# A tiled matmul with bias and residual: one tile per ring slot for the whole kernel, in place of a new tile per use

## The chip, the cores and the metric

One core of a Trainium2 chip. The metric is the device time of one execution in microseconds. The kernel before took 210.93 us (median of 3 runs, 210.77 to 211.21). The span that a profile covers is shorter than the reported time (209.0 against 210.74 us).

## The reference

```python
x: (16, 512, 1024) float32; weight: (1024, 768); bias: (768,); residual: (16, 512, 768)
return (np.matmul(x, weight) + bias + residual).astype(np.float32)
```

Every byte has to move once. x is 33.55 MB, the residual 25.17, the weight 3.15 and the output 25.17, together 87.0 MB. The page of the profile counts 87.2 MB, so the kernel moves nothing twice.

## The kernel before

The 8192 rows of x are 64 row tiles of 128 rows, in 8 blocks of 8 tiles. For each row tile t, ScalarE casts x to bf16 (`xb`), TensorE transposes it as pairs packed in float32 (`pt`, in PSUM), VectorE copies that to SBUF (`xt`), TensorE does 8 contraction steps of two matmuls each (512 and 256 columns) into `po`, and VectorE adds the result to the residual, to which GpSimd has added or will add the bias. All large transfers are issued by SyncE.

Buffers that are used in turn are "rings". Each use of a slot asks the pool for a new tile with the slot's tag; the framework then makes the new tile wait until the old one is retired. A wait is a condition on a semaphore, a counter that other instructions raise. It rides on the instruction that needs it, or it is an instruction of its own, worked off in order by the engine's sequencer, the unit that hands the engine its instructions. A wait whose condition holds when it is reached is called met.

```python
J = 8; HEAD = 3; X_BUFS = 2; RO_BUFS = 4; TMP_BUFS = 4; EARLY = 24; T_STEP = 3
    sb = ctx.enter_context(tc.tile_pool(name="sb", bufs=1))
    ps = ctx.enter_context(tc.tile_pool(name="ps", bufs=1, space=bass.MemoryType.PSUM))

    def ring(pool, name, i, n, shape, dt):
        return pool.tile(shape, dt, name=name, tag=f"{name}{i % n}", bufs=1)

    def psum_o(i):
        return ring(ps, "po", i, HEAD, [P, N], FP32)

    def load_x(S, j0=0, j1=J):
        if S < n_s:
            if j0 == 0:
                x_sb[S] = ring(sb, "x_tile", S, X_BUFS, [P, J, K], FP32)
            K_(nc.sync.dma_start(out=x_sb[S][:, j0:j1, :], in_=x_d[S, :, j0:j1, :]))

    def load_res(S, j0=0, j1=J):
        if S < n_s:
            if j0 == 0:
                ro[S] = ring(sb, "ro", S, RO_BUFS, [P, J, N], FP32)
            K_(nc.sync.dma_start(out=ro[S][:, j0:j1, :], in_=res_d[S, :, j0:j1, :]))
    # [cut: load_w, store, cast]

    def transp(t):
        if t < n_t:
            pt = ring(ps, "pt", t, 2, [P, n_c, P], FP32)
            pairs = xb[t][:, :].bitcast(FP32)
            for c in range(n_c):
                K_(nc.tensor.transpose(
                    out=pt[:, c, :], in_=pairs[:, c * P:(c + 1) * P], identity=ident
                ))
            xt[t] = ring(sb, "xt", t, 4, [P, n_c, P], FP32)
            K_(nc.vector.tensor_copy(out=xt[t], in_=pt))

    def mms(t, i):
        if i == 0:
            po[t] = psum_o(t)
        for n0, nl in chunks:
            mm(t, i, n0, nl)
    # [cut: mm, pool_add, finish, the loads of the start and the first three row tiles]

    for t in range(HEAD, n_t):
        cast(t + 2)
        S, j = divmod(t, J)
        if (t + 2) % J == J - 1:
            if S == 0:
                load_x(X_BUFS, 0, J // 2)
                load_x(X_BUFS, J // 2, J)
            else:
                load_x(S + X_BUFS)
            load_res(S + X_BUFS)
            if 1 <= S < n_s - 1:
                store(S - 1)
        if t < n_t - 1:
            for i in range(len(steps)):
                mms(t, i)
                if i == 0 and t >= n_t - J // 2:
                    finish(t - 1)
                if i == T_STEP:
                    transp(t + 1)
        # [cut: finish, pool_add, the last stores and the last row tile]
```

Of the kernel before, what the change touches and what calls it, by code (L numbers as in the profile page):

```python
# [8 lines left out]
FP32 = mybir.dt.float32  # L9
BF16 = mybir.dt.bfloat16  # L10
P = 128
J = 8
HEAD = 3
X_BUFS = 2
RO_BUFS = 4
TMP_BUFS = 4
# [5 lines left out]
def kernel(  # L22
# [13 lines left out]
    N = weight.shape[1]  # L36
    n_c = K // (2 * P)
# [11 lines left out]
    sb = ctx.enter_context(tc.tile_pool(name="sb", bufs=1))  # L49
    ps = ctx.enter_context(tc.tile_pool(name="ps", bufs=1, space=bass.MemoryType.PSUM))  # L50

    def ring(pool, name, i, n, shape, dt):
        return pool.tile(shape, dt, name=name, tag=f"{name}{i % n}", bufs=1)

    def psum_o(i):
        return ring(ps, "po", i, HEAD, [P, N], FP32)

    x_sb, ro, xb, xt, po, tmp = {}, {}, {}, {}, {}, {}
# [3 lines left out]
# [11 lines that stand above are left out]
# [61 lines left out]
    bias_row = ring(sb, "tmp", TMP_BUFS - 1, TMP_BUFS, [P, N], FP32)  # L134
    K_(nc.gpsimd.memset(bias_row, 0.0))  # L135
    K_(nc.scalar.dma_start(out=bias_row[0:1, :], in_=bias[None, :]))
    w_st = ring(sb, "ro", RO_BUFS - 1, RO_BUFS, [P, n_c, 2, N], FP32)
    w_sb = const.tile([P, n_c, 2, N], BF16, name="w_sb")

    load_x(0, 0, 2)  # L140
# [13 lines left out]

    warm = const.tile([P, 512], BF16, name="warm")
    K_(nc.vector.memset(warm, 0.0))  # L156
    ones = ring(sb, "tmp", 0, TMP_BUFS, [P, P], FP32)
    K_(nc.vector.memset(ones, 1.0))
    warm_a = const.tile([1, 2], FP32, name="warm_a")
    K_(nc.vector.memset(warm_a, 0.0))  # L160
# [123 lines left out]
```

## Time and profile before

| | before |
|---|---|
| median time | 210.93 us |
| TensorE (PE) busy | 200.4 of 209.0 us |
| row tile period on PE, 20 to 199 us | 3.037 us |
| transfers, 20 to 180 us | 428 to 433 GB/s, busy share 1.00 to 1.01 |
| wait instructions on PE | 64 |

The page of the kernel before first: the busy time of PE, the busy share in tenths over 40 slices of the span for PE and for the DMA engines, the chain of waits that ended last, and two groups of instructions (after the bar: busy us, mean ns, idle us before).

```profile
PE 200.4 (96%) x1274; PEld 130.6 (63%) x1299; DVE 105.0 (50%) x139; ACT 67.6 (32%) x68; POOL 115.5 (55%) x71
...
PE   7999999999999999999999999999999999999980
...
DMA  6999999999999999999999999999999999999994
...
PE 96%; issue 1%; DVE 1%
...
L104 PE MATMUL po<-w_sb,xt 128*128 128x512 bf16 (+1 forms) x999 | 175.4, 324 | 1.4
...
L95 PE MATMUL pt<-ident,xb 128*128 128x128 f32 x256 | 38.2, 273 | 0.0
```

Two rows are full, PE and DMA.

The timeline of PE in the kernel before (start, duration, line, what, count):

```profile
98.77 2.76 PE L104 MATMUL po<-w_sb,xt 128*128 128x512 bf16 x16
101.37 0.60 PE L95 MATMUL pt<-ident,xb 128*128 128x128 f32 x4
101.81 2.76 PE L104 MATMUL po<-w_sb,xt 128*128 128x512 bf16 x15
```

From start to start a row tile takes 101.81 - 98.77 = 3.04 us: 2.60 for 16 matmuls, 0.44 for 4 transposes, no gap. (Recorded durations overlap. The x15 is a record lost from the trace: this trace has 1274 of 1299 matmuls.)

The windows of the kernel before, two stretches of 40 us (the last three columns are the granted clock, as a share of TensorE's full one, the DMA busy share and GB/s):

```profile
core 0: us, PE busy (x) PEld busy (x) DVE busy (x) ACT busy (x) POOL busy (x), PEclk, DMA share, GB/s
60.00:100.00 40.00, 39.74 (x261) 26.31 (x264) 20.75 (x28) 13.14 (x14) 30.28 (x17) 1.00 1.01 433
100.00:140.00 40.00, 39.74 (x260) 26.39 (x264) 20.75 (x27) 14.07 (x14) 25.10 (x16) 1.00 1.00 429
```

The instructions of the transpose's line in the kernel before: beside transposes and weight loads it has wait instructions, 51 ns each (a q after an engine's name marks what its sequencer does itself).

```profile
L95 PEldq EVENT_SEMAPHORE  x61: 51/51/51, 6.1 to 196.9; - x61
```

The timeline of SyncE before, from 14 to 24 us: the second residual block, then both halves of the third x block together, then the next residual.

```profile
14.19 0.33 SPq L72 DMA_DIRECT2D ro<-in_residual_dram  x1
22.54 0.81 SPq L66 DMA_DIRECT2D x_tile<-in_x_dram  x2
23.39 0.43 SPq L72 DMA_DIRECT2D ro<-in_residual_dram  x1
```

### The profile page before, as it was taken

How to read it: one execution, taken by the hardware profiler on the slowest of the kernel's cores; microseconds unless marked ns; L12 is line 12 of the kernel's file. 1: busy time of each engine (PE TensorE's matmuls, PEld its weight loads, DVE VectorE, ACT ScalarE, POOL GpSimd, SP SyncE). 2: the span in 40 equal slices, each digit the busy share in tenths (PEclk: the TensorE clock that was granted, in tenths of full speed). 3: DMA queues.
4: the chain of work that ended last, by engine and by line, in shares of the span. 5: the costliest groups of instructions: out<-in, count | busy, mean ns of one | idle time of the engine just before them, and what ended most of it. 6: DMA issues, size and time to landing. Idle time of an engine off the chain costs nothing.

```text
span 209.0 us, 3151 instructions
## 1 busy us (share of the span) xinstructions
PE 200.4 (96%) x1274; PEld 130.6 (63%) x1299; DVE 105.0 (50%) x139; ACT 67.6 (32%) x68; POOL 115.5 (55%) x71
## 2 busy tenths in 40 slices
PE   7999999999999999999999999999999999999980
PEld 2566666666666666666666666666666666666650
DVE  0737465445445544554554455455445544545550
ACT  2544315511723062422443054230724233430000
POOL 2000197819965565999189802994069910799000
PEclk9999999999999999999999999999999999999998
DMA  6999999999999999999999999999999999999994
GB/s 239 427 421 431 436 413 440 442 405 436 423 470 422 419 428 398 459 420 436 433 400 472 416 427 447 412 439 412 437 445 414 445 419 427 442 419 428 426 404 168
DMA packets 5632, 87.23 MB, mean 417 GB/s; under 512 B 625, under 2 KB 753, under 8 KB 1906
## 3 DMA queue, kind: packets, MB, share of 16 engines
q1 hardware_dynamic: 5616, 87.03, 97.9%
q8 instruction: 10, 0.16, 0.3%
q14 instruction: 4, 0.03, 0.0%
q10 hardware_dynamic: 2, 0.00, 0.0%
HBM read 61.87 MB, written 25.17 MB: 416 GB/s over the span
## 4 chain that ended last, share of the span: by engine, by line
PE 96%; issue 1%; DVE 1%
PE po L104 79%; PE pt L95 13%; PE po L170 3%; PE po L190 1%; DVE xt L99 0%; DVE ro L131 0%; DVE warm L156 0%
## 5 line engine op out<-in xcount | busy, mean ns | idle before, releaser
L104 PE MATMUL po<-w_sb,xt 128*128 128x512 bf16 (+1 forms) x999 | 175.4, 324 | 1.4
L104 PEld LDWEIGHTS <-xt 128*128 128x128 bf16 x1024 | 100.1, 98 | 59.5 <-DVE xt L99 0.5
L87 ACT CAST xb<-x_tile 128x1024 bf16<-128x1024 f32 x62 | 62.8, 1044 | 114.5 <-DMA x_tile<-in_x_dram 56.9
L121 POOL TENSOR_TENSOR ro<-ro,bias_sb 128x768 f32<-128x768 f32 x40 | 71.2, 1816 | 36.2 <-DMA ro<-in_residual_dram 26.2
L99 DVE COPY xt<-pt 128x512 f32<-128x512 f32 x64 | 44.2, 691 | 86.7 <-PE pt L95 86.5
L121 POOL TENSOR_TENSOR ro<-ro,tmp 128x768 f32<-128x768 f32 x24 | 43.1, 1814 | 41.0 <-DMA ro<-in_residual_dram 30.2
L131 DVE TENSOR_TENSOR ro<-po,ro 128x768 f32<-128x768 f32 (+2 forms) x41 | 38.0, 930 | 2.9 <-PE po L104 2.8
L95 PE MATMUL pt<-ident,xb 128*128 128x128 f32 x256 | 38.2, 273 | 0.0
L95 PEld LDWEIGHTS pt<-ident,xb 128*128 128x128 f32 x256 | 29.8, 141 | 8.1 <-issue 0.6
L129 DVE TENSOR_TENSOR tmp<-po,bias_sb 128x768 f32<-128x768 f32 x24 | 22.8, 949 | 0.6 <-POOL ro L121 0.5
L170 PE MATMUL po<-warm 128*128 128x512 bf16 x15 | 6.1, 579 | 1.2 <-DVE warm L156 1.2
L176 ACT CAST w_sb<-ro 128x768 bf16<-128x768 f32 x4 | 3.3, 832 | 4.0 <-DMA ro<-in_weight_dram 4.0
L170 PEld LDWEIGHTS <-warm 128*128 128x128 bf16 x15 | 1.9, 135 | 4.1 <-issue 2.8
L87 DVE CAST xb<-x_tile 128x1024 bf16<-128x1024 f32 x2 | 1.4, 696 | 4.8 <-DMA x_tile<-in_x_dram 4.8
L178 DVE CAST w_sb<-ro 128x768 bf16<-128x768 f32 x4 | 2.2, 555 | 2.5 <-DMA ro<-in_weight_dram 2.5
L161 ACT ACT_TABLE_LOAD x1 | 1.3, 1283 | 2.0 <-POOL ident masks.py:199 2.0
L190 PE MATMUL po<-tmp 128*128 128x512 f32 (+1 forms) x4 | 1.5, 486 | 0.0
L198 DVE COPY bias_sb<-po 128x768 f32<-128x768 f32 x1 | 1.0, 958 | 0.1
L190 PEld LDWEIGHTS po<-tmp 128*128 128x128 f32 x4 | 0.7, 190 | 0.5 <-issue 0.5
L135 POOL MEMSET tmp<- 128x768 f32 x1 | 0.7, 737 | 0.3 <-POOLq L268 0.3
L156 DVE MEMSET warm<- 128x256 uint32 x1 | 0.3, 272 | 0.9 <-PEq L268 0.9
masks.py:199 POOL TENSOR_SCALAR_AFFINE_SELECT ident<-ident 128x128 f32<-128x128 f32 x1 | 0.3, 292 | 0.1
(8 smaller groups left out, 1.0 us busy)
## 6 DMA issues: line engine op xcount, KB each, us to landing
ro<-in_residual_dram SPq DMA_DIRECT2D x7, 3072.0 KB, 18.1
out_dram<-ro SPq DMA_DIRECT2D x7, 3072.0 KB, 23.9
x_tile<-in_x_dram SPq DMA_DIRECT2D x5, 4096.0 KB, 30.8
x_tile<-in_x_dram SPq DMA_DIRECT2D x4, 2048.0 KB, 27.6
x_tile<-in_x_dram SPq DMA_DIRECT2D x3, 1024.0 KB, 8.6
ro<-in_weight_dram SPq DMA_DIRECT2D x4, 768.0 KB, 9.0
ro<-in_residual_dram SPq DMA_DIRECT2D x2, 1536.0 KB, 21.1
out_dram<-ro SPq DMA_DIRECT2D x1, 1536.0 KB, 11.9
```

Of the source, the lines that this page charges most:

```text
L87: K_(copy(out=xb[t], in_=x_sb[t // J][:, t % J, :]))
L95: K_(nc.tensor.transpose(out=pt[:, c, :], in_=pairs[:, c * P:(c + 1) * P], identity=ident))
L99: K_(nc.vector.tensor_copy(out=xt[t], in_=pt))
L104: K_(nc.tensor.matmul(po[t][:, n0:n0 + nl], lhsT=both[:, e, :], rhs=w_sb[:, c, e, n0:n0 + nl], start=(i == 0), stop=(i == len(steps) - 1),))
L121: K_(nc.gpsimd.tensor_add(out=r, in0=r, in1=tmp[t] if t < EARLY else bias_sb))
L129: K_(nc.vector.tensor_add(out=tmp[t], in0=p, in1=bias_sb))
L131: K_(nc.vector.tensor_add(out=row(t, n0, nl), in0=p, in1=row(t, n0, nl)))
L161: K_(nc.scalar.copy(out=warm_a, in_=warm_a))
L170: K_(nc.tensor.matmul(warm_ps[:, 0:512], lhsT=warm[:, 0:P], rhs=warm, start=True, stop=True))
L176: K_(nc.scalar.copy(out=w_sb[:, c, e, :], in_=w_st[:, c, e, :]))
L178: K_(nc.vector.tensor_copy(out=w_sb[:, c, e, :], in_=w_st[:, c, e, :]))
L190: K_(nc.tensor.matmul(bias_ps[:, n0:n0 + nl], lhsT=ones, rhs=bias_row[:, n0:n0 + nl], start=True, stop=True,))
```

## The change

The intent: a ring slot stays the same memory throughout, so let it be one tile object. Dependencies are then found between accesses that overlap in that tile, instead of between all accesses of a retired tile and its successor. A load into half a slot need then wait only for the readers of that half, and waits that only the handover from tile to tile needs can go.

```diff
+    fixed = {}
+
     def ring(pool, name, i, n, shape, dt):
-        return pool.tile(shape, dt, name=name, tag=f"{name}{i % n}", bufs=1)
+
+        key = f"{name}{i % n}"
+        if key not in fixed:
+            fixed[key] = pool.tile(shape, dt, name=key)
+        return fixed[key]
[...]
-    w_st = ring(sb, "ro", RO_BUFS - 1, RO_BUFS, [P, n_c, 2, N], FP32)
+    w_st = ring(sb, "ro", RO_BUFS - 1, RO_BUFS, [P, J, N], FP32).rearrange(
+        "p (c e) n -> p c e n", e=2
+    )
[...]
-    ones = ring(sb, "tmp", 0, TMP_BUFS, [P, P], FP32)
+    ones = ring(sb, "tmp", 0, TMP_BUFS, [P, N], FP32)[:, 0:P]
```

The last two edits give users of a slot the slot's one shape. In the built programs every engine has the same instructions in the same order, and every SBUF tile has the same address; only waits differ.

## The prediction

> **What bounds the kernel now.** TensorE. The page shows PE busy 96% of the 209.0 us span; the chain that ended last is 96% PE (79% main matmuls, 13% transposes). In PE's timeline one row tile follows another every 3.037 us from 20 us to 199 us: 16 main matmuls, 2.60 us, then 4 transposes, 0.44 us. The groups show 1.4 us idle before all main matmuls, none before transposes. DMA is a close second: the windows from 20 to 180 us show share 1.00, 428 to 433 GB/s. Waits for it (ACT for x 56.9 us, GpSimd for the residual 56.4 us, in the waits view) are absorbed by buffers. Only a shorter PE period, head (about 20 us) or tail (6 us) could help.
>
> **What the change does.** I compared the built programs. Every engine has the same instructions in the same order, and every tile the same address. Only semaphore waits differ, because dependencies are now found between overlapping accesses of one long-lived tile, not between a retired tile and its successor.
>
> 1. PE loses its waits on its own semaphore (about two per row tile, on much earlier PE work), and with them 59 of 64 wait instructions. The Trainium skill (Perfetto Trace Analysis, Identifying Dependency Chains) says an instruction with several waits may get EventSemaphore instructions before it; this trace agrees: 61 at the transposes, 51 ns each. Naively 59 x 51 ns = 3.0 us. I give it zero: they run 1.6 us ahead of their transposes. Between matmul starts of the 109 ns kind, the mean is 109.19 ns where one falls in between (57 cases), 109.18 ns where none does (599).
> 2. The first half of the third x block may be loaded once rows 0 to 3 of its slot are cast, not all eight. Its issue moves from 22.5 us to about 16.3 us (the cast of row 3 starts at 15.47 us and takes 0.70). The second half still waits for row 7, so it and all later issues stay. Gain: nil, it only queues. Packet sizes in the trace follow issue order, and the loads issued ahead of it, about 10 MB at 22.5 us, last until about 46 us. The skill (DMA: Bandwidth & Descriptors, Queues, rings and completion order) says an engine consumes descriptors in ring order; these packets agree.
> 3. GpSimd gains waits on long finished adds (2 more wait instructions). It is busy 55%, and its late adds run ahead of their users. DVE drops four waits on stores that its other waits imply. Critical path: zero.
>
> Final stores, three-tile head and one-tile tail are untouched.
>
> **Predicted time.** 210.9 us, against 210.93 before; 8 times in 10 between 210.3 and 211.5. Chances: faster by over 2% 0.01, within 2% 0.98, slower by over 2% 0.01.
>
> **What would show each step.** (1) Wait instructions on PE fall from 64 to about 5, the tile period stays 3.037 us. If they cost PE, it falls to about 2.99 and the span by about 3 us. (2) In SyncE's timeline the pair of x issues at 22.5 us splits: one at about 16.3, one at 22.5; the median landing of the 2 MB x loads grows; casts of block 2 start as before. (3) GpSimd's adds keep 1.82 us each. The chain stays 96% PE, traffic 87.2 MB.
>
> **What would make it wrong.** Wait instructions cost PE's front end in a way that start-to-start times hide; the early x half interleaves with the loads ahead of it, so the first residual (now 25.5 us) lands later and DVE, held by the four-slot ring, holds PE; self-waits on GpSimd delay its adds until stores and loads slip. None should reach 2%.

## The result, and the profile after

| | before | after |
|---|---|---|
| median time, same rounds | 210.86 us (4 runs) | 210.81 us (4 runs, 210.56 to 210.94) |
| ratio of fast runs | | 0.9993, 95% interval 0.9976 to 1.0011 |
| wait instructions on PE | 64 | 5 |
| row tile period on PE | 3.037 us | 3.037 us |
| first half of third x block issued | 22.5 us | 16.4 us |
| the same, landed | 51.2 us | 51.3 us |

Ratios here and below are the mean time of one kernel's fast runs over that of the other's fast runs of the same rounds, so not quite the ratio of the medians that are quoted.

The lines of the page after that answer to those of before. In this trace tiles keep their slot's number, so groups are split by slot and are not shown.

```profile
PE 201.9 (97%) x1299; PEld 130.6 (62%) x1299; DVE 105.0 (50%) x139; ACT 67.6 (32%) x68; POOL 115.6 (55%) x71
...
DMA  6999999999999999999999999999999999999994
...
PE 96%; DVE 1%; issue 0%
```

PE's busy time seems to have grown by 1.5 us. It has not: this trace holds all 1299 matmuls, the other lacked 25. Compare counts before you compare busy times.

The timeline of PE after:

```profile
98.96 1.46 PE L110 MATMUL po_101<-w_sb,xt_130 128*128 128x512 bf16 x8
100.26 1.46 PE L110 MATMUL po_157<-w_sb,xt_141 128*128 128x512 bf16 x8
101.56 0.60 PE L101 MATMUL pt_125<-ident,xb_154 128*128 128x128 f32 x4
102.00 1.46 PE L110 MATMUL po_157<-w_sb,xt_141 128*128 128x512 bf16 x8
```

102.00 - 98.96 = 3.04 us: the same period, with (the next line, the transposes of the program after) 2 wait instructions left there of 61:

```profile
L101 PEldq EVENT_SEMAPHORE  x2: 51/51/51, 6.3 to 7.8; - x2
```

The timeline of SyncE after. The merged row of two issues begins at 16.39 us and ends at 23.00; the second of the two issues stands at 22.7 us.

```profile
14.33 0.33 SPq L78 DMA_DIRECT2D ro_85<-in_residual_dram  x1
16.39 6.61 SPq L72 DMA_DIRECT2D x_tile_69<-in_x_dram  x2
23.05 0.43 SPq L78 DMA_DIRECT2D ro_269<-in_residual_dram  x1
```

The transfer of that half, from the DMA view (KB, us from issue to landing), first before, then after, each followed by ScalarE's casts that use it:

```profile
x_tile<-in_x_dram SPq DMA_DIRECT2D x1, 2048.0 KB, 28.7
...
51.29 3.89 ACT L87 CAST xb<-x_tile 128x1024 bf16<-128x1024 f32 x4 [8.49 <-DMA x_tile<-in_x_dram]
```

```profile
x_tile_69<-in_x_dram SPq DMA_DIRECT2D x1, 2048.0 KB, 34.9
...
51.34 1.05 ACT L93 CAST xb_114<-x_tile_69 128x1024 bf16<-128x1024 f32 x1 [8.31 <-DMA x_tile_69<-in_x_dram]
```

22.54 + 28.7 = 51.2 and 16.39 + 34.9 = 51.3: issued 6.15 us earlier, landed at the same time. The load only waited in the transfers' queue rather than in SyncE. The windows after are those of before:

```profile
60.00:100.00 40.00, 40.00 (x265) 26.39 (x264) 20.75 (x28) 13.32 (x14) 30.20 (x18) 1.00 1.01 431
100.00:140.00 40.00, 40.00 (x265) 26.31 (x264) 20.75 (x27) 14.08 (x14) 25.28 (x16) 1.00 1.01 430
```

### The profile page after: what moved, and what is told of

The parts are those of the page before. It is cut to its first block, busy times and chain, and to the rows that moved or that the text cites. A ratio compares the mean times of both kernels' runs of the same rounds, so it can differ in the third digit from the quotient of the medians.

```text
span 209.1 us, 3119 instructions
## 1 busy us (share of the span) xinstructions
PE 201.9 (97%) x1299; PEld 130.6 (62%) x1299; DVE 105.0 (50%) x139; ACT 67.6 (32%) x68; POOL 115.6 (55%) x71
## 3 DMA queue, kind: packets, MB, share of 16 engines
q1 hardware_dynamic: 5616, 87.03, 97.8%
## 4 chain that ended last, share of the span: by engine, by line
PE 96%; DVE 1%; issue 0%
PE po_157 L110 27%; PE po_100 L110 27%; PE po_101 L110 26%; PE pt_118 L101 7%; PE pt_125 L101 7%; PE po_100 L178 3%; PE po_101 L198 1%; DVE xt_208 L105 0%; DVE ro_67 L137 0%; DVE warm L164 0%
## 5 line engine op out<-in xcount | busy, mean ns | idle before, releaser
L127 POOL TENSOR_TENSOR ro_67<-ro_67,bias_sb 128x768 f32<-128x768 f32 x16 | 28.5, 1822 | 11.5 <-DMA ro_67<-in_residual_dram 11.5
L110 PEld LDWEIGHTS <-xt_208 128*128 128x128 bf16 x256 | 25.0, 98 | 15.3 <-DVE xt_208 L105 0.5
L110 PEld LDWEIGHTS <-xt_123 128*128 128x128 bf16 x256 | 25.1, 98 | 14.8
L110 PEld LDWEIGHTS <-xt_130 128*128 128x128 bf16 x256 | 25.0, 98 | 14.8
L110 PEld LDWEIGHTS <-xt_141 128*128 128x128 bf16 x256 | 25.1, 98 | 14.7
L105 DVE COPY xt_123<-pt_118 128x512 f32<-128x512 f32 x16 | 11.1, 692 | 22.7 <-PE pt_118 L101 22.7
L105 DVE COPY xt_141<-pt_118 128x512 f32<-128x512 f32 x16 | 11.1, 692 | 21.7 <-PE pt_118 L101 21.7
L105 DVE COPY xt_130<-pt_125 128x512 f32<-128x512 f32 x16 | 11.1, 691 | 21.3 <-PE pt_125 L101 21.3
L105 DVE COPY xt_208<-pt_125 128x512 f32<-128x512 f32 x16 | 11.1, 692 | 20.9 <-PE pt_125 L101 20.7
L93 ACT CAST xb_114<-x_tile_81 128x1024 bf16<-128x1024 f32 x8 | 8.4, 1046 | 37.9 <-DMA x_tile_81<-in_x_dram 32.0
L127 POOL TENSOR_TENSOR ro_269<-ro_269,bias_sb 128x768 f32<-128x768 f32 x8 | 14.2, 1826 | 10.0 <-DMA ro_269<-in_residual_dram 10.0
L127 POOL TENSOR_TENSOR ro_85<-ro_85,bias_sb 128x768 f32<-128x768 f32 x8 | 14.2, 1822 | 10.0 <-DMA ro_85<-in_residual_dram 10.0
L110 PE MATMUL po_100<-w_sb,xt_130 128*128 128x512 bf16 x96 | 17.9, 326 | 0.0
L110 PE MATMUL po_101<-w_sb,xt_141 128*128 128x512 bf16 x96 | 17.9, 326 | 0.0
L110 PE MATMUL po_157<-w_sb,xt_123 128*128 128x512 bf16 x96 | 17.9, 326 | 0.0
L127 POOL TENSOR_TENSOR ro_79<-ro_79,tmp_89 128x768 f32<-128x768 f32 x2 | 3.6, 1812 | 25.2 <-DMA ro_79<-in_residual_dram 25.2
L93 ACT CAST xb_114<-x_tile_69 128x1024 bf16<-128x1024 f32 x7 | 7.3, 1046 | 29.9 <-DMA x_tile_69<-in_x_dram 21.4
L127 POOL TENSOR_TENSOR ro_79<-ro_79,bias_sb 128x768 f32<-128x768 f32 x8 | 14.2, 1821 | 4.7 <-DMA ro_79<-in_residual_dram 4.7
L110 PE MATMUL po_157<-w_sb,xt_208 128*128 128x512 bf16 x88 | 16.5, 331 | 0.1
L110 PE MATMUL po_100<-w_sb,xt_208 128*128 128x512 bf16 (+1 forms) x88 | 15.7, 321 | 0.0
L110 PE MATMUL po_101<-w_sb,xt_123 128*128 128x512 bf16 x80 | 14.6, 326 | 0.0
L110 PE MATMUL po_101<-w_sb,xt_130 128*128 128x512 bf16 x80 | 14.6, 326 | 0.0
```

Source lines behind the costliest of these rows:

```text
L93: K_(copy(out=xb[t], in_=x_sb[t // J][:, t % J, :]))
L110: K_(nc.tensor.matmul(po[t][:, n0:n0 + nl], lhsT=both[:, e, :], rhs=w_sb[:, c, e, n0:n0 + nl], start=(i == 0), stop=(i == len(steps) - 1),))
L127: K_(nc.gpsimd.tensor_add(out=r, in0=r, in1=tmp[t] if t < EARLY else bias_sb))
```

## The experiments

The questions: do 59 wait instructions really cost nothing, or was a gain of 3 us lost elsewhere? Do the two halves of the change cancel? And is it PE that kept both kernels at the same time? Twelve kernels were run.

### Adding waits to PE: e1, e2, e3, e9

Waits on a semaphore that is met from the start are put before matmuls of the changed kernel. The builder folds some of them into other instructions, so the count that matters is that of separate wait instructions, checked in the program. They are the same kind of instruction as the removed ones, recorded with the same 51 ns. The added ones are met when they are reached; the 61 at the transposes of the kernel before are on much earlier PE work and start 1.6 us (median) ahead of their transposes.

```diff
+    sem_x = nc.alloc_semaphore(name="extra_wait")
[...]
         for n0, nl in chunks:
+            if t >= HEAD and WHERE:
+                for _ in range(COUNT):
+                    K_(nc.tensor.wait_ge(sem_x, 0))
             mm(t, i, n0, nl)
```

e1: WHERE is `i % 2 == 0 and n0 == 0`, COUNT 2. e2: always, 2. e3: always, 4. e9: always, 4 for the first chunk and 2 for the second.

> The changed kernel with 4 added wait instructions on TensorE per row tile (240 in all, each met from the start), four times what the change removed. Theory (a met wait is worked off by PE's sequencer ahead of the matmuls, so it costs nothing while the sequencer keeps ahead): tile period 3.037 us, time 210.8 us, within 0.3. Rival (every wait instruction holds PE for its 51 ns, and the 3.0 us that the change saved were lost elsewhere): 240 x 51 ns = 12.2 us, so about 223 us and a tile period of 3.24 us.

> As e1, with 16 added wait instructions per row tile (960 in all). Theory: if every instruction takes PE's sequencer about 51 ns as a wait does (an estimate), 40 of them plus 16 waits take 56 x 51 ns = 2.86 us, below the tile period of 3.037 us, so still about 211 us. Rival: 960 x 51 ns = 49 us, about 260 us.

> As e1, with 32 added wait instructions per row tile (1920 in all): meant to overrun the sequencer, to show that the waits do cost once there is no slack. Theory, by the same estimate: 72 x 51 ns = 3.67 us per tile in place of 3.037, so 39 us more, about 250 us. Rival: 1920 x 51 ns = 98 us more, about 309 us.

| run | added per row tile | median | ratio to before (95%) | period on PE |
|---|---|---|---|---|
| e1 | 4 | 211.38 us | 1.0012 (0.9996 to 1.0028) | 3.037 us |
| e2 | 16 | 211.09 us | 1.0004 (0.9989 to 1.0019) | 3.037 us |
| e3 | 32 | 257.0 us | 1.218 (1.2161 to 1.2198) | 3.85 us (mean) |

960 added waits cost nothing; the rival, 51 ns for each, would be 260 us. 1920 cost 46 us. So there is a slack, and past it waits cost. The timeline of PE with 32 waits per tile shows a stretched tile (this one takes 3.95 us, the mean is 3.85), and the waits view a new entry: idle time of the weight loads for which nothing but issue is to blame (us in total, times, longest).

```profile
100.91 0.60 PE L102 MATMUL pt<-ident,xb 128*128 128x128 f32 x4
101.35 3.67 PE L111 MATMUL po<-w_sb,xt 128*128 128x512 bf16 x16
104.86 0.60 PE L102 MATMUL pt<-ident,xb 128*128 128x128 f32 x4
```

```profile
PEld L111 <- issue: 22.0, 115, 0.3
```

My estimate for e3 (250 us) came out near the truth for a wrong reason. The single records of PE in the e3 trace, start in ns:

```
100128 wait   100234 wait   100311 weight load   100342 matmul (256 columns)
100360 wait   100466 wait   100543 weight load   100573 matmul (512 columns)
100592 wait   100698 wait   ...
```

From one wait to the next are 106 ns (100128 to 100234), or 126 ns where a load and a matmul stand in between (100234 to 100360). So a wait takes about 106 ns of PE's sequencer, and a load and matmul together only about 20; I had given 51 to each. (The pair's 20 ns include the added waits that were folded into it.) For a tile with 32 waits and 20 pairs that makes 32 x 0.106 + 20 x 0.020 = 3.79 us; 3.85 was measured. The Trainium skill (Perfetto Trace Analysis, Per-instruction lifecycle, Sequencer-only Instruction) says that for an instruction of this kind the profile reports only its execution, and not the wait, the push of the semaphore update and its propagation. This trace agrees: 51 ns recorded of 106 taken; what fills the other 55 is not shown. By these numbers (an estimate) the slack ends at (3.037 - 0.40) / 0.106 = 25 waits per tile. The two estimates part at 24:

> The changed kernel with 24 added wait instructions per row tile (1440 in all). In the trace with 32 waits per tile, PE is held by its sequencer: a wait follows a wait after 106 ns, and after 126 ns where a weight load and a matmul stand between them. So a wait takes about 106 ns of the sequencer, of which the record shows 51, and a load and a matmul together 20. Refined theory: 24 x 106 ns + 20 x 20 ns = 2.94 us per tile, just below 3.037, so 211 us (at most 214). The earlier estimate (51 ns for every instruction of PE): 64 x 51 ns = 3.26 us per tile, so about 224 us.

e9 took 211.12 us, ratio 0.9999 (0.9975 to 1.0023), period 3.037 us. The old estimate, 224 us, is refuted. Its waits on PE, from the view of their line:

```profile
L122 PEldq EVENT_SEMAPHORE  x1440: 51/51/51, 16.6 to 199.9; - x180
```

Twenty-four times as many waits as the kernel before had per tile, 73 us if one added up their records, and no cost.

### Half of the change undone: e4, e5

```diff
     def ring(pool, name, i, n, shape, dt):
+        if pool is ps:      # e4; in e5: pool is sb
+            return pool.tile(shape, dt, name=name, tag=f"{name}{i % n}", bufs=1)
         key = f"{name}{i % n}"
```

> Half of the change undone: the two PSUM rings are newly allocated at each use again, the SBUF rings stay fixed. The built program has the 64 PE wait instructions of before and every other wait as after the change. Theory: 210.8 us, ratio to before 1.000 within 0.002, tile period 3.037 us, first half of the third x block issued at 16.4 us and landed at 51.3 us. Rival (the two halves of the change have effects that cancel: PE gains 3 us, the memory side loses 3 us): this half keeps the loss and gives up the gain, so about 214 us.

> The other half undone: the SBUF rings are newly allocated at each use again, the PSUM rings stay fixed. The built program has 5 PE wait instructions as after the change, and the memory-side waits of before. Theory: 210.9 us, ratio to before 1.000 within 0.002, tile period 3.037 us, first half of the third x block issued at 22.5 us and landed at 51.2 us. Rival (halves that cancel): this half keeps PE's gain without the loss, so about 208 us.

e4 took 211.15 us, ratio 1.0008 (0.9996 to 1.0021); e5 211.21 us, ratio 1.0015 (0.9998 to 1.0031). The halves part cleanly. For e4, then for e5, the waits on the transposes' line and the issue of the third x block:

```profile
L102 PEldq EVENT_SEMAPHORE  x61: 51/51/51, 6.5 to 197.3; - x61
...
16.60 6.63 SPq L73 DMA_DIRECT2D x_tile<-in_x_dram  x2
```

```profile
L102 PEldq EVENT_SEMAPHORE  x2: 51/51/51, 6.2 to 7.7; - x2
...
22.68 0.95 SPq L73 DMA_DIRECT2D x_tile<-in_x_dram  x2
```

e4 has the waits and the early issue, e5 neither. Both run like the kernel before (the rival needed 214 and 208 us). Of the two times only e4's is a test: a loss of 3 us on the memory side would have shown there. A gain of 3 us on PE could not have shown in e5's time, for e6 below takes as much from PE and is no faster. That PE gained nothing is read from its tile period, 3.037 us in before, after, e4 and e5. So nothing is cancelled by anything.

### Taking work from PE: e6, e7, e8

One of the 8 contraction steps is left out in some row tiles; the result is wrong.

```diff
             for i in range(len(steps)):
-                mms(t, i)
+                if i != 6 or not (t % 6 == 0):     # e6; in e7 and e8: every t of this loop
+                    mms(t, i)
```

> The changed kernel with one of the 8 contraction steps left out in every sixth row tile (10 tiles; wrong result on purpose): takes 10 x 0.325 us = 3.25 us of matmuls from PE, about what 59 x 51 ns would have been. Theory (PE's matmul time is what binds, and the wait instructions never were part of it): the time falls by nearly all of it, to 207.6 us (down to 208.3 if the transfers catch up at the end). Rival (the transfers bind as well, and swallow any saving on PE, so a saving from the waits could not have shown): 210.8 us.

> The kernel before with one of the 8 steps left out in every row tile but the first three and the last (60 tiles; wrong result on purpose): takes 19.5 us from PE, so that the transfers bind. Theory: 87.0 MB at 430 GB/s are 202.4 us; with the 2 us before the first bytes and the last store's 2 to 4 us the time should be 206 to 208 us, not 191.

> The same cut in the changed kernel. Theory (the earlier issue only queues behind transfers already issued): the same as e7 within 0.4 us. Rival (the finer waits on memory do help, and PE's bound hid it): faster than e7 by 1 us or more, as the transfers now bind.

| run | taken from PE | median | ratio to before (95%) |
|---|---|---|---|
| e6, on after | 3.25 us | 211.07 us | 1.0001 (0.9986 to 1.0016) |
| e7, on before | 19.5 us | 210.75 us | 0.9991 (0.9976 to 1.0006) |
| e8, on after | 19.5 us | 210.72 us | 0.9987 (0.9972 to 1.0002) |

Here my theory fell: e6 should have been 207.6 us and was unchanged, and even 19.5 us less on PE bought nothing that is clear of the noise. In e6 the mean tile period did fall to 2.987 us and the last matmul starts at 200.0 us in place of 203.0, but the last store takes 7.8 us to land in place of 4.6. The page of e8 shows the same full DMA row, and its chain now runs through transfers:

```profile
DMA  6999999999999999999999999999999999999994
...
DMA 70%; PE 18%; ACT 2%; SPq 2%; issue 1%; DVE 1%; ACTq 0%
```

PE now waits for data while the transfers run no faster than before, 429 to 432 GB/s from 20 to 180 us in e7 and e8. From the views of e8: a window, PE's waits for ScalarE's casts (us in total, times, longest), and two row tiles' matmuls out of the chain (start, us), the first of them after a stall:

```profile
140.00:180.00 40.00, 36.69 (x229) 23.12 (x231) 19.90 (x27) 14.41 (x15) 19.97 (x12) 0.96 1.00 430
...
PE pt L102 <- ACT xb L94: 7.6, 5, 2.2
...
172.53 3.58 PE po L111 x14
176.54 2.27 PE po L111 x14
```

ScalarE's casts wait for x (77.0 us in all). The 3.58 us show a second loss: from 172.5 to 176.1 us, after PE had stood still for 2.2 us, the granted clock was 0.65, and matmuls of 512 columns started 427 ns apart in place of 216. Two such stretches cost e8 about 3.3 us, one cost e7 about 1.4 us. This does not explain the result: the last matmul of e7 and e8 still starts 7 to 8 us sooner than without the cut.

The end of the kernel shows how a PE that is done sooner gains nothing. The last stores in the DMA view, KB and us to landing: first after, then e8.

```profile
out_dram<-ro_67 SPq DMA_DIRECT2D x1, 384.0 KB, 5.6
out_dram<-ro_67 SPq DMA_DIRECT2D x1, 256.0 KB, 4.8
out_dram<-ro_67 SPq DMA_DIRECT2D x1, 128.0 KB, 4.6
```

```profile
out_dram<-ro SPq DMA_DIRECT2D x1, 384.0 KB, 12.0
out_dram<-ro SPq DMA_DIRECT2D x1, 256.0 KB, 11.2
out_dram<-ro SPq DMA_DIRECT2D x1, 128.0 KB, 11.0
```

In e8 SyncE issues them some 6 us earlier (its issues end at 197.9 us against 204.1), and they land 6 us later after issue, because transfers issued before them are still moving. The packets of the main queue span 206.0 us in the trace of before, 206.2 after and 205.7 in e8. My 206 to 208 us for e7 were too low because 430 GB/s is the rate of the middle only: over the 205.9 us of packets in e7's trace the mean is 87.03 MB / 205.9 us = 423 GB/s, and the reported time of its profiled run is 1.8 us above the span (210.59 against 208.8).

e7 and e8 differ by 0.03 us. With the transfers binding, the earlier issue of the changed kernel still gives nothing.

### Taking work from the transfers, and from both: e10, e11, e12

The residual of blocks 4 to 6 is not loaded, the slots keep what they held (wrong).

```diff
     def load_res(S, j0=0, j1=J):
         if S < n_s:
+            if S in (4, 5, 6):
+                ro[S] = ro[S - RO_BUFS]
+                return
```

> The changed kernel without the residual loads of blocks 4, 5 and 6 (the slots keep what they held; wrong result on purpose): 9.44 MB or 22 us less for the transfers at 430 GB/s, PE's work whole. The runs with a shorter PE did not get faster, against what I had forecast, so the transfers bind as well. If both bind (PE has no idle time between 9.5 and 203 us, and the transfers none either): 210.5 us, within 0.5. If the transfers alone bind and PE only looks full: about 190 us.

> The changed kernel with both cuts, 19.5 us off PE and 22 us off the transfers (wrong on purpose). If both bind: about 191 us, that is 19 to 20 us less, limited by PE again. If something else holds the kernel at 209 us (an order of waits, a fixed cost): no change.

> The kernel before with both cuts (wrong on purpose). With the two bounds lowered, a gain from fewer PE wait instructions or from finer waits would have room to show. Theory (neither is worth anything): the same as e11 within 0.5 us. Rival (59 waits of 51 to 106 ns hold PE): e12 slower than e11 by 3 to 6 us.

| run | taken from PE | taken from the transfers | median | ratio to before (95%) |
|---|---|---|---|---|
| e10, on after | 0 | 22 us | 208.61 us | 0.9882 (0.9863 to 0.9902) |
| e11, on after | 19.5 us | 22 us | 192.36 us | 0.9114 (0.9095 to 0.9132) |
| e12, on before | 19.5 us | 22 us | 192.34 us | 0.9115 (0.9093 to 0.9137) |

22 us less traffic alone gives 2.5 us. I had expected about half a microsecond; the rest sits in the tail. PE runs as before, row tile period 3.037 us and last matmul started at 203.2 us (203.0 after the change), but the last stores of e10 find the queue empty:

```profile
out_dram<-ro SPq DMA_DIRECT2D x1, 384.0 KB, 2.4
out_dram<-ro SPq DMA_DIRECT2D x1, 256.0 KB, 2.0
out_dram<-ro SPq DMA_DIRECT2D x1, 128.0 KB, 1.9
```

The last one lands 2.7 us sooner than after the change (1.9 in place of 4.6). Both cuts together give 18 to 19 us. So two resources bind at once: PE up to its last matmul, and the transfers, whose backlog also makes the tail. Neither cut alone is worth much, both are worth nearly the smaller. The cut loads also take with them SyncE's waits for the stores that had to leave their slots first, so e10 to e12 alone can't tell bytes from the order of waits; that it is the bytes is read from e7 and e8, where PE stalled and the transfers stayed at share 1.00.

And with both bounds lowered the kernel before and the changed one still take the same, 192.34 and 192.36 us. For the waits on PE this is the clearest test of the change itself. In e11 PE still stalls for data before 100 us (it is busy for 38.75 and 37.74 us of the two windows of 40 us from 20 us on) and works through after that. About 32 row tiles lie there; at 51 to 106 ns for a wait a gain of 1.6 to 3.4 us would have shown (an estimate), and there is none. The early load had no such room: the transfers of e11 and e12 still run at share 1.00 or 1.01 from 20 to 140 us. That it is worth nothing is shown for a full queue only.

## Why the prediction was right or wrong

The time was right: 210.9 us predicted, 210.81 measured, and "within 2%" held. Points 1 to 3 earned it; point 4 was wrong and did no harm, because a change that gives nothing to PE or to the transfers takes the same time whichever of them binds. In that the number was lucky. Point by point:

1. Wait instructions on PE. Right, 64 to 5 and the period stays 3.037 us. That they cost nothing is shown by e1, e2 and e9 (up to 24 more per tile without effect), by e4, and by e12 against e11. That it is for slack in PE's sequencer is shown by e3, where the slack ends. The naive cost, 51 ns each, was mis-sized as well: a wait takes about 106 ns, of a sequencer that has about 2.6 us per tile to spare for waits (an estimate, from the spacing in e3).
2. The earlier issue. Right: 16.39 us against about 16.3 predicted, the second half at 22.7, landing at 51.3 against 51.2 us. Behind a full queue it brought nothing, and e8 against e7 shows the same with PE out of the way.
3. GpSimd and VectorE. Right but for a count: GpSimd has 17 wait instructions for 15, adds of 1.82 us, 55% busy; e4 (17) and e5 (15) differ in these waits and not in time. On VectorE the instructions of the kept traces carry three wait conditions fewer (211 to 208), not four.
4. "What bounds the kernel now. TensorE" with the DMA as "a close second" whose waits "are absorbed by buffers", and "Only a shorter PE period, head (about 20 us) or tail (6 us) could help". This step failed. A PE with 19.5 us less to do took the same time (e7, e8). PE and transfers bind together: with both cut, 192.4 us. And the waits are absorbed only while PE has as much to do as before: in e8 PE stood still for 7.6 us for ScalarE's casts, which waited for x.
5. "If they cost PE, it falls to about 2.99 and the span by about 3 us". The second half of this check was wrong: e6 took 3.25 us from PE, which showed in the mean tile period (2.987 us) and not in the time. Had the waits cost 3 us, their removal should have looked the same. So the unchanged time alone proves nothing about the waits; the period and the added waits do.

The trace had said so. The windows give 428 to 433 GB/s at share 1.00 to 1.01 for 160 us, and the Trainium skill (Perfetto Trace Analysis, Roofline) puts the limit of a single core at its 16 DMA engines, about 435 GB/s in all. This trace agrees with that figure: no window of 40 us shows more than 433, and e7 and e8, where PE left room, show no more than 432. I had read the share as "second" because the chain named PE alone.

Left open: one row tile, near 32 us, takes 0.03 to 0.05 us longer than its neighbours in several of the runs, after the change among them, and not in before, e4, e9 or e10. It is worth nothing in the time, and was not followed up.

No version that beats both kernels came out of this. Every byte already moves once and takes 206 us of packets, and PE works from 9.5 to 203 us with one gap, of 0.14 us. Less traffic alone gave 2.5 us (e10), less of both 18 to 19 us; none of the runs does either with a right result.

## What to carry to other kernels

Here a met wait that TensorE's sequencer reached ahead of the work cost nothing until the sequencer itself was full (24 per tile free, 32 not): count waits per period and compare their real spacing with the period, before you remove any. An earlier issue behind a full queue brought nothing (51.3 against 51.2 us); compare landings, not issues. When two rows of the page are full, do not rank them by the chain: shorten one, then the other, then both, and see which moves the time.

## What the Trainium skill lacked or had wrong

- What a met wait instruction costs on TensorE's sequencer (belongs to Perfetto Trace Analysis, Per-instruction lifecycle; the page says what is hidden but has no number): 106 ns from wait to wait, 51 of it recorded, against about 20 ns for a weight load and matmul together; 24 per 3.037 us tile free, 32 not (3.85 us).
- That a wait instruction with slack is free (belongs to Perfetto Trace Analysis, Identifying Dependency Chains, which says only that such instructions may be inserted): 59 fewer gave a ratio of 0.9993 (0.9976 to 1.0011), 1440 more 0.9999 (0.9975 to 1.0023).
- Identifying the Most-Contended Engine, on the same page, speaks of one most-contended engine, and not of two that bind at once. Here they do: cutting one alone gave 0.3 us, which is within the noise (19.5 us off PE), or 2.5 us (22 us off the transfers), cutting both 19 us.
- DMA: Bandwidth & Descriptors, Queues, rings and completion order, agrees with the runs: a load issued 6.15 us earlier behind a full queue landed 0.1 us apart. How much a backlog adds to the last store has no page that I know of: the last 128 KB store took 4.6 us behind a backlog, 1.9 us without one.
